# Low part of the feed-forward weights: an accumulating DMA instead of a VectorE subtraction

## The chip, the cores and the metric

The kernel runs on one core of a Trainium2 chip. The metric is device time of one launch in microseconds (us). The engines that matter are TensorE (PE in the rows: matmuls; PEld: its weight loads), VectorE (DVE), ScalarE (ACT), GpSimd (POOL) and SyncE (SP, which only issues DMAs). Each engine works through its own list of instructions in order and meets the others at semaphores.

## What is computed

Two layers of a diffusion transformer on 640 tokens (512 latent, 128 context) of width 1024, in float32: layer 0 mixes tokens with an mLSTM and a Hyena convolution, layer 1 with attention. After each mixer stands a feed-forward block, and that is where the change lies:

```python
def conv_ffn(h, w_up, w_conv, w_down):
    a, g = jnp.split(h @ w_up, 2, axis=-1)
    return (jax.nn.gelu(dwconv3(a, w_conv)) * g) @ w_down
```

Here `w_up` is 1024 x 5632 and `w_down` 2816 x 1024. The input of the block is an RMS norm with conditioning; its output, gated, is added to the residual stream `x`.

## The kernel before

**Exact products.** TensorE multiplies in a reduced format (fp32r). Each float32 operand is therefore split in two such parts, W = Wh + Wl, and a product takes three matmuls: Wh·Xh, Wh·Xl and Wl·Xh. For weights, `split_w` (lines 94 to 99) does this: ScalarE rounds the raw block to Wh (line 97), VectorE subtracts it from the raw block to give Wl (line 98).

**Tiles.** A weight tile is 128 partitions x 1024 float32 (512 KB; 896 columns in the second and third group of `w_down`): eight k-blocks of 128 x 128 for 128 output features. The three stages of a tile are `raw` (four buffers, loaded by SP, line 103), `wh` and `wl` (three buffers each). A tile's buffers come free with its last matmul, so the split of tile i + 3 can start when tile i ends, and is needed two tiles later.

**The block's loops.** `ffn` takes the 22 blocks of 128 inner features in three groups. For each, `up` runs `linear` over the tiles of `w_up` (a and g in turn), then `linear` runs over eight tiles of `w_down`, whose products are added to `x`. Ordinary tiles run one by one through `mm_k` (for each k the three matmuls on both halves of the tokens, the Wl matmul last; lines 118 to 123). Two places differ:

- The head: the first three tiles of `w_up` (`u_0` to `u_2`; a tile u is named by the place of its group's first tile and its own number in it) run together, by halves of the tokens, because the norm before them delivers its result bit by bit. GpSimd makes their low parts. They hold all three `wh` and `wl` buffers until they end, nearly together, so `u_3` can be split only then, and is the next tile that TensorE needs.
- The tail: the last three tiles of `w_down` (`d_5` to `d_7` of the third group) run half by half, so each of them stands only half as long before the next.

While layer 0's block runs, VectorE also computes the conditioning of what follows (`ada_dve`, line 247), from 512 KB loads per step.

**Order.** The order on each engine's list is fixed when the program is built: the framework places instructions by their dependences and its own estimates of time. `conv3`, the GELU, its product and the split of that product (`fcb`, `ge`, `pr`, `G` in the rows) share ScalarE and VectorE with the weight splits.

Of the kernel before, what the change touches and what calls it, by code (L numbers as in the profile page):

```python
# [36 lines left out]
def trunk(ctx: ExitStack, tc: tile.TileContext, I, O, dbg=None, stop=None):  # L37
# [7 lines left out]
    def use_psum(pairs, singles):  # L45
        """the 8 banks of PSUM: so many tiles of two banks and of one"""
        if "es" in psum:
            psum["es"].close()
        es = psum["es"] = ExitStack()
        psum["shape"] = pairs, singles  # L50
        n = psum["n"] = psum.get("n", 0) + 1
        kw = dict(space=bass.MemoryType.PSUM, reuse_waits="tile")
        psum["m"] = es.enter_context(tc.tile_pool(name=f"pm{n}", bufs=pairs, **kw))
        psum["s"] = es.enter_context(tc.tile_pool(name=f"ps{n}", bufs=singles, **kw))
# [7 lines left out]
    def bank(pt, a):  # L62
        """half a of a tile of two banks, or of two tiles of one"""
        return pt[a] if isinstance(pt, tuple) else pt[:, a]

    # ---------------------------------------------------------------- constants and persistent data
# [21 lines left out]
    # ---------------------------------------------------------------- weights: load, exact split  # L88
# [11 lines left out]

    def load_w(src, nm, nk=KT, eng=dve):
        raw = wp.tile([P, 1024], F32, tag="raw", name=nm, bufs=4)
        sp.dma_start(out=raw[:, : nk * P], in_=src)
        wh, wl = split_w(raw, nk * P, nm, eng)
        return wh.rearrange("p (k c) -> p k c", c=P), wl.rearrange("p (k c) -> p k c", c=P)
# [19 lines left out]
    def linear(srcs, done, nm, ks=None, nk=KT, head=2, tail=0, by_half=True, split=SPLIT, filler=None,  # L125
               kcut=None, pre=(), hook=None, spare=False, pooled=(), x_last=False):
        """ks: (k index in the weight tile, xh, xl) in the order of arrival; head: so many first tiles run with
        k outermost; tail: so many last ones finish half by half; spare: the tile after the head in single banks;
        x_last: in the head, the low parts of the tokens come after those of the weights"""
# [4 lines left out]
        while i < n:  # L134
            left = n - i
            g = min(head, left) if i == 0 and head else (tail if tail and left == tail else 1)
            # while a norm holds the vector engine
            eng = pool if i == 0 and head and by_half or i in pooled else dve
# [40 lines left out]
    # tokens on partitions: out[tile] = X[:, tile]^T W, W 512 columns wide  # L179
# [17 lines left out]
    # ---------------------------------------------------------------- adaLN modulation  # L197
# [10 lines left out]
    # on the tensor engine, two blocks (chunk, half of it) of 512 features at once; in four steps  # L208
# [29 lines left out]
    # on the vector engine: rows of W^T times the conditioning vectors; list of steps, one per 128 features  # L238
# [17 lines left out]
    # ---------------------------------------------------------------- RMSNorm (+ adaLN), by halves of the tokens  # L256
    # (start, end, request group) of each half, and overlapping windows of 128 tokens that cover it
# [6 lines left out]
    def rms_steps(nm, a, nrm):  # L264
        """1/rms of the tokens of half a, in every partition of a PSUM tile; in two steps"""
# [18 lines left out]
        # one Newton step of 1/sqrt  # L284
# [26 lines left out]
    def norm_steps(l, which, nrm):  # L311
        """both halves, in seven steps for the end of the product before it"""
# [22 lines left out]

    # ---------------------------------------------------------------- depthwise conv of width 3 along tokens
    # buffers: a column of padding, 512 latent tokens, padding, 128 context tokens, padding
    def halves(pt):
        """both halves of PSUM: the columns that are latent in both, and those latent in the first only"""
        return pt[:, :, 0 : NS - HT], pt[:, :, NS - HT : HT]  # L340

    def conv_parts(buf, d):
        """the same columns of a buffer, moved by d"""
        e = 1 if d > 1 else 0
        return (buf[:, 0 : 2 * HT].rearrange("p (a b) -> p a b", a=2)[:, :, d : d + NS - HT],
                buf[:, e : e + 2 * HT + 2].rearrange("p (a b) -> p a b", a=2)[:, :, NS - HT + d - e : HT + d - e])
# [9 lines left out]
    def tokens(buf):  # L356
        """(slice of the tokens, their columns of a buffer)"""
# [14 lines left out]
    # ---------------------------------------------------------------- ConvFFN  # L372
    def ffn(l, after, hook=None):
        with ExitStack() as es:
# [43 lines left out]
            def up(i0, i1):  # L418
                linear([I["w_up"][l, i // 2, i % 2] for i in range(i0, i1)], lambda i, pt, a: done_up(i0 + i, pt, a),
                       f"u{l}_{i0}_", head=3 if i0 == 0 else 0, filler=filler, spare=i0 == 0)  # L420

            nxt = 0
            for gi, (k0, k1) in enumerate(GROUPS):
                end = 2 * min(k1 + 1, NF)
                if end > nxt:
# [5 lines left out]
                       tail=3 if k1 == NF else 0, hook=hook)  # L431

    # ---------------------------------------------------------------- hyena filters (no data from x)
    def hyena_filters(fl, spectra):
        """in three parts: the loads, the filters, their spectra"""
# [18 lines left out]
        # the decay, where the first of the products with it will be  # L454
# [5 lines left out]
        for j, w in enumerate((w1, w2)):  # L460
# [18 lines left out]
            if j == 0:  # L479
                # sum and difference of the two filters' weights, twice (64 rows each), and their exact split  # L480
# [5 lines left out]
        # high parts of the hidden layer, then low parts  # L486
# [6 lines left out]
        for r in range(5):  # L493
# [8 lines left out]
            if r in (0, 4):  # L502
                # the filter of the future has no tap at 0: half of sum plus difference
# [34 lines left out]
    # ---------------------------------------------------------------- mixers A and B  # L538
    def mixer_ab():
        with ExitStack() as es:  # L540
# [9 lines left out]
            # weight tiles: (v, x1) x 4, x2 x 4, gates, q x 4, k x 4, o x 4  # L550
# [73 lines left out]
            # x holds u, then the convolved u (tiles 0-3), and x2, then y of the hyena (tiles 4-7)  # L624
            def hyena_chunk(j):
# [42 lines left out]
                # context sequence  # L668
# [64 lines left out]
            # running maxima: high parts from rows 0 and 32, low parts 64 rows further; and columns that pick both  # L733
# [7 lines left out]
            def mlstm_gates(pt, rows):  # L741
# [24 lines left out]
                # log_sigmoid(f) = min(f, 0) - log(u) + ((u - 1) - e), u = fl(1 + e)  # L766
# [79 lines left out]
            def head_a(h):  # L846
                q, k = qk[:, h], qk[:, 4 + h]
                # latent sequence
# [33 lines left out]
                # context sequence  # L882
# [19 lines left out]
            def head_b(h):  # L902
# [25 lines left out]
                # norm per head: rstd = exp(-ln(v)/2) and one Newton step  # L928
# [53 lines left out]
    # ---------------------------------------------------------------- mixer C  # L982
    # latent tokens of keys, values and queries go column by column of the grid: token c * 8 + r
    def mixer_c():
        with ExitStack() as es:
# [6 lines left out]
            # context keys of a head, the other head's rows zero  # L992
            kc = [[at.tile([P, P], F32, name=f"kc{b}{e}") for e in range(2)] for b in range(2)]
            # latent keys between 64 columns of padding, the high part twice and the low part once: with the queries
            # as (high, low) they give all products but low times low
            k1 = [[at.tile([P, 640], F32R, name=f"k1{b}{e}") for e in range(2)] for b in range(2)]
            k2 = [[at.tile([P, 640], F32R, name=f"k2{b}{e}") for e in range(2)] for b in range(2)]
            # 64 columns of padding, 512 latent tokens, 64 columns of padding, 128 context tokens
# [13 lines left out]
            # PSUM (rows 0-4 | rows 5-7, context) to column order  # L1012
# [300 lines left out]
def pack(i):  # L1313
# [10 lines left out]
    # (chunk, k pair, half, p, par, 512) and, for the other chunks, transposed (chunk, tile, p, 1024)  # L1324
# [44 lines left out]
    # rpbw[8 b + r, h, 8 a + r2]: bias of query (row r, column c) and key (row r2, column c + a - b - 8)  # L1369
# [45 lines left out]
```

## Time and profile before

| | |
|---|---|
| time, median of 3 runs | 1732.03 us (1731.26 to 1732.91) |
| span of the profiled execution | 1733.2 us |
| TensorE busy | 1676.1 us, 97% |
| VectorE busy | 1052.3 us, 61% |
| ScalarE busy | 672.4 us, 39% |
| GpSimd busy | 142.2 us, 8% |
| DMA moved | 175.62 MB, mean 101 GB/s |

The profiled execution's span lies 1.2 us above the median of the runs. A busy TensorE is not TensorE at its peak, since matmuls overlap: what matters is where its list stands still, and for whom. Idle time of the other engines costs nothing as long as TensorE does not wait for it.

### The profile page before, as it was taken

What the parts mean: (1) busy time and instruction counts of PE and PEld (TensorE: products, weight loads), DVE (VectorE), ACT (ScalarE), POOL (GpSimd) and SP (SyncE); (2) the same over time, 40 slices, a digit from 0 to 9 for tenths busy, and PEclk for the clock granted to TensorE, in tenths of its full rate; (3) what the DMA queues carried; (4) which work ended last, traced back from release to release, by engine and by line L of the source; (5) the groups of instructions that cost most, each with busy time, mean ns of one, the idle gap of its engine ahead of it and who ended that gap; (6) DMA issues with size and microseconds to landing.
All of it is one profiled execution on the core that took longest, in us unless ns stands there. A gap on an engine that the chain in (4) does not pass through costs nothing. (4 is left out here: it accounts for less than half of the span.)

```text
span 1733.2 us, 28191 instructions
## 1 busy us (share of the span) xinstructions
PE 1676.1 (97%) x11434; PEld 1596.5 (92%) x11434; DVE 1052.3 (61%) x2089; ACT 672.4 (39%) x1235; POOL 142.2 (8%) x150
## 2 busy tenths in 40 slices
PE   5999999999999999999997999999999999999997
PEld 2699889899999999999997888998999999999997
DVE  5886656666987677777376555555564433433444
ACT  6323346754432133223245565555343312321332
POOL 3110001101000000000023212120100000000001
PEclk9999999999999999999999999999999999999998
DMA  8334422141454454453213111211222222222211
GB/s 325 117 132 163 160 72 71 48 142 59 140 176 147 146 153 144 154 170 104 79 64 101 60 60 47 65 42 52 74 73 74 73 74 73 71 76 85 69 54 61
DMA packets 57121, 175.62 MB, mean 101 GB/s; under 512 B 7632, under 2 KB 15104, under 8 KB 56736
## 3 DMA queue, kind: packets, MB, share of 16 engines
q1 hardware_dynamic: 56800, 173.66, 31.1%
q8 instruction: 90, 1.47, 0.4%
q14 instruction: 39, 0.32, 0.1%
q0 software_dynamic: 192, 0.17, 0.0%
HBM read 169.61 MB, written 4.20 MB: 100 GB/s over the span
## 5 line engine op out<-in xcount | busy, mean ns | idle before, releaser
L331 DVE SCALAR_TENSOR_TENSOR x<-pd,mod,x 128x320 f32<-128x320 f32 (+2 forms) x144 | 55.1, 434 | 146.7 <-PE pd L122 137.3
L247 DVE CUSTOM_DVE_ANT_0 adj<-adw,cb 128x1024 f32<-128x1024 f32 x112 | 136.7, 1221 | 1.6
L398 DVE TENSOR_TENSOR pr<-pu,ge 128x384 f32<-128x384 f32 x84 | 37.4, 486 | 108.4 <-PE pu L122 107.6
L353 DVE SCALAR_TENSOR_TENSOR fcb<-pu,cwf,fcb 128x384 f32<-128x384 f32 (+1 forms) x176 | 95.8, 549 | 4.1
L388 ACT ACTIVATE ge<-fcb 128x641 f32<-128x641 f32 x44 | 32.6, 742 | 105.4 <-DVE fcb L353 105.4
L306 ACT ACTIVATE XH<-nt,mod 128x192 fp32r<-128x192 f32 (+1 forms) x96 | 39.6, 466 | 44.0 <-DVE nt L302 43.8
L1120 DVE CUSTOM_DVE_ANT_0 s<-pS,bm 128x384 f32<-128x384 f32 x64 | 34.5, 553 | 30.1 <-PE pS L1119 29.0
L307 DVE SCALAR_TENSOR_TENSOR XL<-nt,mod,XH 128x192 fp32r<-128x192 f32 (+1 forms) x96 | 46.4, 521 | 5.0 <-ACT XH L306 4.9
L1021 DVE TENSOR_SCALAR s<-s,nm 128x384 f32<-128x384 f32 (+1 forms) x80 | 46.3, 586 | 1.8
L1019 ACT ACTIVATE s<-s,nm 128x384 f32<-128x384 f32 x64 | 39.2, 612 | 20.3 <-DVE nm L1120 18.3
L350 ACT ACTIVATE fcb<-pu,cwf 128x384 f32<-128x384 f32 x88 | 46.3, 528 | 1.3
L1194 POOL TENSOR_TENSOR fo<-fo,rs 128x320 f32<-128x320 f32 x8 | 6.9, 888 | 469.8 <-ACT rs L1186 469.8
L1134 ACT COPY pTs<-pS 128x384 f32<-128x384 f32 (+1 forms) x80 | 33.7, 434 | 23.4 <-PE pS L1132 22.7
L1132 PE MATMUL pS<-ident,s 128*128 128x128 f32 x208 | 36.3, 281 | 5.8 <-DVE s L1021 5.8
L98 POOL TENSOR_TENSOR qk00l<-qk,qk00h 128x1024 fp32r<-128x1024 f32 x1 | 2.8, 2761 | 461.6 <-DVE rn L288 461.6
L273 ACT ACTIVATE sqn<-x 128x320 f32<-128x320 f32 x56 | 25.3, 466 | 39.4 <-DVE x L331 35.3
L1094 POOL TENSOR_TENSOR bm<-amask,wr 128x768 f32<-128x768 f32 x16 | 30.7, 1918 | 112.6 <-issue 83.9
L302 DVE SCALAR_TENSOR_TENSOR nt<-x,coefA,rbn 128x192 f32<-128x192 f32 (+1 forms) x96 | 36.7, 430 | 3.6 <-PE rbn L294 3.5
L1112 PE MATMUL pS<-k,q 128*128 128x256 f32 x128 | 31.0, 328 | 7.6 <-DVE k L1047 7.1
L400 ACT CAST G<-pr 128x640 fp32r<-128x640 f32 x44 | 31.8, 728 | 13.4 <-DVE pr L398 13.4
L331 DVE SCALAR_TENSOR_TENSOR x<-pop,mod,x 128x320 f32<-128x320 f32 (+2 forms) x36 | 14.4, 433 | 36.7 <-PE pop L122 26.0
L401 DVE TENSOR_TENSOR G<-pr,G 128x640 fp32r<-128x640 f32 x44 | 36.0, 819 | 0.0
(1110 smaller groups left out, 5507.4 us busy)
## 6 DMA issues: line engine op xcount, KB each, us to landing
u<-in_w_up SPq DMA_DIRECT2D x88, 512.0 KB, 3.5
adw<-in_w_adaT SPq DMA_DIRECT2D x56, 512.0 KB, 4.1
wa<-in_w_ada SPq DMA_DIRECT2D x40, 512.0 KB, 5.0
d<-in_w_down SPq DMA_DIRECT2D x32, 448.0 KB, 3.3
qk<-in_w_qkv SPq DMA_DIRECT2D x24, 512.0 KB, 3.5
d<-in_w_down SPq DMA_DIRECT2D x16, 512.0 KB, 3.5
qk<-in_w_ab SPq DMA_DIRECT2D x8, 512.0 KB, 3.5
op<-in_w_oab SPq DMA_DIRECT2D x6, 512.0 KB, 3.4
```

Source lines behind the costliest of these rows:

```text
L247: dve.tensor_tensor_reduce(out=jk, in0=w, in1=cb[:, s], op0=ALU.mult, op1=ALU.add, scale=1.0, scalar=0.0, accum_out=acc[:, k, s : s + 1])
L302: dve.scalar_tensor_tensor(out=t, in0=x[:, k, c0:c1], scalar=coefA[:, n, k, s : s + 1], in1=rb[:, c0 - a * HT : c1 - a * HT], op0=ALU.mult ...
L306: act.activation(out=oh, in_=t, func=AF.Identity, bias=b)
L307: last = dve.scalar_tensor_tensor(out=ol, in0=t, scalar=b, in1=oh.bitcast(F32), op0=ALU.add, op1=ALU.subtract)
L331: r = dve.scalar_tensor_tensor(out=x[:, k, c0:c1], in0=pt[:, h, c0 - h * HT : c1 - h * HT], scalar=mod[:, l, ch, k, s : s + 1], in1=x[:, k ...
L350: act.activation(out=o, in_=i, func=AF.Copy, scale=w[1])
L353: dve.scalar_tensor_tensor(out=o, in0=i, scalar=w[j], in1=o, op0=ALU.mult, op1=ALU.add)
L398: dve.tensor_tensor(out=o, in0=i_, in1=c, op=ALU.mult)
L401: here[0] = dve.tensor_tensor(out=g[:, 1], in0=pr, in1=g[:, 0].bitcast(F32), op=ALU.subtract).ins
L1019: act.activation(out=s, in_=src, func=AF.Exp, scale=-1.0, bias=nm, accum_out=sm)
L1021: dve.tensor_scalar(out=s, in0=s, scalar1=sm, scalar2=None, op0=ALU.mult)
L1132: pe.transpose(pS[:, j * P : (j + 1) * P], s[:, j * P : (j + 1) * P], ident)
```

## The change

A second form of the split, `split_dma`, is used for all tiles of the feed-forward block but the three of the head (82 tiles of `w_up` and 48 of `w_down` in the two layers, 130 in all). ScalarE rounds the raw block to Wh as before, then writes -Wh into `wl`, and a DMA issued by GpSimd adds the raw block in SBUF onto it, in place. VectorE has no part in it any more.

```diff
+    def split_dma(raw, n, nm):
+
+        wh = wp.tile([P, 1024], F32R, tag="wh", name=f"{nm}h")
+        wl = wp.tile([P, 1024], F32R, tag="wl", name=f"{nm}l")
+        act.copy(out=wh[:, :n], in_=raw[:, :n])
+        act.activation(out=wl[:, :n], in_=wh[:, :n].bitcast(F32), func=AF.Copy, scale=-1.0)
+        pool.dma_start(out=wl[:, :n], in_=raw[:, :n], accum_op=ALU.add)
+        return wh, wl
...
-        wh, wl = split_w(raw, nk * P, nm, eng)
+        wh, wl = split_w(raw, nk * P, nm, eng) if eng is not None else split_dma(raw, nk * P, nm)
...
-            eng = pool if i == 0 and head and by_half or i in pooled else dve
+            eng = pool if i == 0 and head and by_half or i in pooled else (None if by_dma else dve)
...
-                       f"u{l}_{i0}_", head=3 if i0 == 0 else 0, filler=filler, spare=i0 == 0)
+                       f"u{l}_{i0}_", head=3 if i0 == 0 else 0, filler=filler, spare=i0 == 0, by_dma=True)
...
-                       tail=3 if k1 == NF else 0, hook=hook)
+                       tail=3 if k1 == NF else 0, hook=hook, by_dma=True)
```

The lists of instructions change with it; lines from 100 on have other numbers afterwards (line 97 becomes 105 here, 122 becomes 131, 350 becomes 359, 273 becomes 282). ScalarE at the end of the head in layer 0, before: `u_0_3h` is Wh of tile `u_3`, `fcb` the convolution's buffer, `pu` a tile's result.

```order
L97 CAST u_0_3h<-u_0_3_4314 128x1024
L350 ACTIVATE fcb_4094<-pu_0_0_4127,cwf_4092 128x2x192
L97 CAST u_0_4h<-u_0_4_4383 128x1024
L350 ACTIVATE fcb_4094<-pu_0_0_4127,cwf_4092 128x2x128
L350 ACTIVATE fcb_4095<-pu_0_2_4129,cwf_4092 128x2x192
L97 CAST u_0_5h<-u_0_5_4452 128x1024
```

The same place now.

```order
L105 CAST u_0_3h<-u_0_3_4314 128x1024
L359 ACTIVATE fcb_4094<-pu_0_0_4127,cwf_4092 128x2x192
L106 ACTIVATE u_0_3l<-u_0_3h 128x1024
L359 ACTIVATE fcb_4094<-pu_0_0_4127,cwf_4092 128x2x128
L359 ACTIVATE fcb_4095<-pu_0_2_4129,cwf_4092 128x2x192
L105 CAST u_0_4h<-u_0_4_4384 128x1024
L359 ACTIVATE fcb_4095<-pu_0_2_4129,cwf_4092 128x2x128
L106 ACTIVATE u_0_4l<-u_0_4h 128x1024
```

Each rounding has a negation (line 106) behind it, one instruction of the convolution between them; the DMA of `u_3` can be issued after the third row. TensorE's list at the first matmuls of `u_3` in layer 0, before; a bracket names the semaphores that a row waits for.

```order
L122 MATMUL pu_0_3_0_4320<-XH,u_0_3h 128x320 [waits Activation_49]
L122 MATMUL pu_0_3_1_4321<-XH,u_0_3h 128x320 [waits PE_49]
L122 MATMUL pu_0_3_0_4320<-XL,u_0_3h 128x320
L122 MATMUL pu_0_3_1_4321<-XL,u_0_3h 128x320
L122 MATMUL pu_0_3_0_4320<-XH,u_0_3l 128x320 [waits DVE_49]
L122 MATMUL pu_0_3_1_4321<-XH,u_0_3l 128x320
```

The same place now.

```order
L131 MATMUL pu_0_3_0_4321<-XH,u_0_3h 128x320 [waits Activation_49]
L131 MATMUL pu_0_3_1_4322<-XH,u_0_3h 128x320 [waits PE_49]
L131 MATMUL pu_0_3_0_4321<-XL,u_0_3h 128x320
L131 MATMUL pu_0_3_1_4322<-XL,u_0_3h 128x320
L131 MATMUL pu_0_4_4391<-XH,u_0_4h 128x320 [waits DVE_49,PE_49,Activation_49]
L131 MATMUL pu_0_4_4391<-XH,u_0_4h 128x320
L131 MATMUL pu_0_3_0_4321<-XH,u_0_3l 128x320 [waits DMASW6_49]
L131 MATMUL pu_0_3_1_4322<-XH,u_0_3l 128x320
```

The first Wl matmul waits for a DMA of GpSimd's queue (DMASW) in place of VectorE, and two matmuls of `u_4` have moved ahead of it. The other matmuls keep their order. ScalarE in the tail of layer 1, before, where `sqfin` are squares for the last norm.

```order
L97 CAST d_2_6h<-d_2_6_16318 128x896
L273 ACTIVATE sqfin_16430<-x 128x320
L97 CAST d_2_7h<-d_2_7_16324 128x896
L273 ACTIVATE sqfin_16433<-x 128x320
L273 ACTIVATE sqfin_16436<-x 128x320
```

The same place now.

```order
L105 CAST d_2_6h<-d_2_6_16446 128x896
L282 ACTIVATE sqfin_16560<-x 128x320
L106 ACTIVATE d_2_6l<-d_2_6h 128x896
L105 CAST d_2_7h<-d_2_7_16453 128x896
L282 ACTIVATE sqfin_16563<-x 128x320
L106 ACTIVATE d_2_7l<-d_2_7h 128x896
L282 ACTIVATE sqfin_16566<-x 128x320
```

The negation of `d_7` stands behind a square. GpSimd's list holds, after the subtractions of the head's three tiles, nothing but the accumulating DMAs of that layer.

## Rows read from the trace of the kernel before

**Rows 1.** The page: busy time of each engine.
```profile
PE 1676.1 (97%) x11434; PEld 1596.5 (92%) x11434; DVE 1052.3 (61%) x2089; ACT 672.4 (39%) x1235; POOL 142.2 (8%) x150
```

**Rows 2.** Stretches (start:end, length, busy PE, PEld, DVE, ACT, POOL, clock, DMA share, GB/s).
```profile
442.00:887.00 445.00, 445.00 (x3035) 444.41 (x3033) 323.34 (x545) 129.61 (x174) 4.88 (x2) 1.00 0.45 139
1274.00:1718.00 444.00, 444.00 (x3032) 444.00 (x3031) 188.21 (x310) 126.44 (x169) 0.00 (x0) 1.00 0.23 71
```

**Rows 3.** Timeline, ordinary tile, layer 1 (start, duration, engine, line, [idle before <- releaser]).
```profile
1399.94 1.05 ACT L97 CAST d_5h<-d 128x1024 fp32r<-128x1024 f32 x1 [5.99 <-PE pd L122]
1401.28 1.22 DVE L98 TENSOR_TENSOR d_5l<-d,d_5h 128x1024 fp32r<-128x1024 f32 x1
...
1413.97 0.63 PEld L122 LDWEIGHTS pd<-G,d_5h 128*128 128x128 f32 x4
```

**Rows 4.** Timeline, end of the head in layer 0.
```profile
439.39 1.05 ACT L97 CAST u_3h<-u 128x1024 fp32r<-128x1024 f32 x1 [1.19 <-PE pu L116]
440.35 0.58 ACT L350 ACTIVATE fcb<-pu,cwf 128x384 f32<-128x384 f32 x1
440.48 1.23 DVE L98 TENSOR_TENSOR u_3l<-u,u_3h 128x1024 fp32r<-128x1024 f32 x1 [1.89 <-ACT u_3h L97]
...
441.94 0.46 PE L122 MATMUL pu<-XH,u_3l 128*128 128x320 f32 x2
442.23 0.46 PE L122 MATMUL pu<-XH,u_3h 128*128 128x320 f32 x2
```

**Rows 5.** Timeline, end of the head in layer 1.
```profile
1271.35 1.05 ACT L97 CAST u_3h<-u 128x1024 fp32r<-128x1024 f32 x1 [1.25 <-PE pu L116]
...
1273.90 0.46 PE L122 MATMUL pu<-XH,u_3l 128*128 128x320 f32 x2
```

**Rows 6.** Timeline, tails of layer 0 and of layer 1.
```profile
866.29 0.94 ACT L97 CAST d_7h<-d 128x896 fp32r<-128x896 f32 x1 [4.75 <-PE pd L122]
...
867.23 0.47 ACT L273 ACTIVATE sqn<-x 128x320 f32<-128x320 f32 x1
867.64 1.08 DVE L98 TENSOR_TENSOR d_7l<-d,d_7h 128x896 fp32r<-128x896 f32 x1
...
872.84 0.31 PE L116 MATMUL pd<-G,d_7l 128*128 128x320 f32 x1
...
1698.25 0.94 ACT L97 CAST d_7h<-d 128x896 fp32r<-128x896 f32 x1 [4.75 <-PE pd L122]
...
1704.80 0.31 PE L116 MATMUL pd<-G,d_7l 128*128 128x320 f32 x1
```

**Rows 7.** DMA issues (queue, count, KB each, median us from issue to landing).
```profile
u<-in_w_up SPq DMA_DIRECT2D x88, 512.0 KB, 3.5
adw<-in_w_adaT SPq DMA_DIRECT2D x56, 512.0 KB, 4.1
...
kctx<-in_k_ctx SPq DMA_DIRECT2D x1, 1024.0 KB, 4.9
...
out_ck<-kc SPq DMA_DIRECT2D x16, 32.0 KB, 1.8
...
selc<-in_k_selc POOLq DMA_DIRECT2D x1, 2.0 KB, 3.1
...
cwq<-in_w_conv_qk POOLq DMA_DIRECT2D x1, 12.0 KB, 5.1
```

**Rows 8.** TensorE around its longest wait, by microseconds (length, busy PE, clock, DMA).
```profile
923.00:924.00 1.00, 0.00 (x0) 0.65 1.23 333
...
925.00:926.00 1.00, 0.54 (x2) 0.50 0.41 164
...
930.00:931.00 1.00, 1.00 (x9) 0.94 0.00 0
```

**Rows 9.** Timeline: the wait that rows 8 show.
```profile
925.46 0.77 PE L1112 MATMUL pS<-k,q 128*128 128x256 f32 x2 [7.11 <-DVE k L1047]
```

**Rows 10.** Timeline: VectorE behind the head of layer 0.
```profile
444.81 3.36 DVE L353 SCALAR_TENSOR_TENSOR fcb<-pu,cwf,fcb 128x256 f32<-128x256 f32 x7
```

More of the change, by code (lines that the diff above doesn't have):

```diff
@@ L125, in linear @@
     def linear(srcs, done, nm, ks=None, nk=KT, head=2, tail=0, by_half=True, split=SPLIT, filler=None,
-               kcut=None, pre=(), hook=None, spare=False, pooled=(), x_last=False):
+               kcut=None, pre=(), hook=None, spare=False, pooled=(), x_last=False, by_dma=False):
         n = len(srcs)
```

## The prediction

> **What bounds the kernel now.** I read the page's busy times first: TensorE 1676.1 of 1733.2 us, VectorE 61%, ScalarE 39%, GpSimd 8% [rows 1]. Then the two stretches that the change touches, from the first tile after each head to the end of the tail: TensorE is busy for 445.00 of 445.00 us in layer 0 and 444.00 of 444.00 in layer 1, at a granted clock of 1.00 [rows 2]. So in the whole feed-forward block TensorE's list is the time, and nothing that VectorE does there is waited for, though it is busy for 323.34 us of layer 0's stretch [rows 2]. Taking work off VectorE can gain nothing in these 889 us. What is left to ask is only whether the new way of making Wl is ever late.
>
> The timeline of an ordinary tile shows how much time there is: d_5 is rounded from 1399.94, VectorE has its low part at 1401.28 + 1.22 = 1402.50, and TensorE's first weight load of it is at 1413.97 [rows 3]. That is 14.03 us (two tiles) after the start of the split, and the first Wl matmul comes another 0.6 us later. At the end of the heads it is otherwise: u_3 is rounded from 439.39, its low part is ready at 440.48 + 1.23 = 441.71, and the first matmul that reads it starts at 441.94 [rows 4]: 0.23 us to spare. In layer 1 the same pair is 1271.35 and 1273.90, again 2.55 us apart [rows 4, 5]. In the tails d_7 is rounded from 866.29 and read at 872.84, and from 1698.25 and 1704.80: 6.55 us apart both times [rows 6].
>
> **Removed: 130 subtractions on VectorE**, 1.22 us each [rows 3], some 150 us in all. Nothing on TensorE's path ended on them in the two stretches, so this is worth 0. In the heads the subtraction of u_3 was on time by 0.23 us; what takes its place is next.
>
> **Added on ScalarE: 130 negations.** They read and write as many elements as the rounding, so I take its 1.05 us (0.94 for 896 columns) [rows 3, 6]; on ScalarE, busy for 129.61 of 445 us [rows 2], they are hidden in ordinary tiles. If they came late they would hold up the rounding of the tile after, which has 14 us. Cost 0, but for the two places where they stand ahead of a late DMA.
>
> **Added on GpSimd: 130 accumulating DMAs.** The trace has no such DMA. Call L the time from its issue to its landing, bounded by the nearest rows. GpSimd's own DMAs, all small, land in 3.1 us (2 KB) to 5.1 us (12 KB, in the crowded start) against 1.8 us for 32 KB on SP's queue [rows 7]. Another 512 KB adds 1.4 us (4.9 for 1024 KB against 3.5 for 512 KB) [rows 7]. An accumulation has to read two blocks and write one. Low end: 3.1 + 1.4 = 4.5 us, as if the second read were free. High end: 5.1 + 3 x 1.4 = 9.3 us, every pass in series on the slowest start. I take the small DMA's 3.1 and two passes: L = 3.1 + 2.8 = 5.9 us, because the reads are what an accumulation doubles, and GpSimd's queue will be as empty as for the 2 KB row. For 896 columns it is 3.1 + 2 x 1.2 = 5.5 us.
>
> [...]
>
> **Ordinary tiles.** Rounding, up to one convolution instruction, negation: the DMA goes out at most 1.05 + 0.58 + 1.05 = 2.7 us after the start of the split and lands at 2.7 + 5.9 = 8.6 us, of 14.6 that there are. Hidden up to L = 11.9 us. The raw buffer is held 6 us longer, so SP's next loads go out later, and the loads of the conditioning queue behind them; raw has four buffers, four tiles or 28 us, so this costs 0 too.
>
> **Heads.** ScalarE does u_3's rounding, the convolution until 440.93, then the negation until 441.98 [rows 4]. The DMA lands at 441.98 + 5.9 = 447.9. TensorE wants it at 441.94 [rows 4]; two matmuls of u_4, which the new list puts ahead, fill 0.3 us. Idle: 447.9 − 441.94 − 0.3 = 5.6 us, or L less 0.3. Behind it everything is shifted, u_4 included: its own DMA goes out two convolution instructions, a rounding and a negation later, about 3.3 us, and a tile takes 7. To this comes the clock. In the longest wait of TensorE, 7.11 us until 925.46 [rows 9], the granted clock fell at about 923.3 (a mean of 0.65 is 0.3 us at 1.00 and 0.7 at 0.50), 5.0 us after the last work, and came back at about 930.1, 4.7 us after work began again [rows 8]. [...] A wait of 5.6 us is just past those 5.0, so I count it: 7.9 us for each head, 15.8 for both. Without the fall it is 11.2.
>
> **Tails.** d_7's rounding ends at 867.23, the square at 867.70, the negation at 868.64; the DMA lands at 868.64 + 5.5 = 874.14 where TensorE wants it at 872.84 [rows 6]: 1.3 us, twice, 2.6 us. For d_6 and d_5 there are 3 and 6 us more, so nothing. The end of the kernel hangs on the last tile's result and moves with it.
>
> **The sum.** 15.8 + 2.6 = 18.4 us onto a span of 1733.2, 1751.6; the profiled span lies 1.2 us above the median of the runs, so 1750.4 us. With the bounds of L: at 4.5 us the heads wait 4.2 us each, without a fall of the clock, and the tails nothing, 8.4 us in all: 1740.4. At 9.3 us the heads cost 9.0 + 2.3 each and the tails (8.8 us for 896 columns) 4.6 each, 31.8 in all: 1763.8.
>
> **Rivals.**
> 1. The DMA engines fill up in layer 0. They are busy for 0.45 there [rows 2], 3.2 us of each 7.04 us tile, since the conditioning is loaded beside the weights (56 loads of 512 KB in all [rows 7]); 3.8 us are free. If an accumulation occupies them for three passes of 1.4 us, 4.2 us, each tile with such a load takes 0.4 us longer: 56 x 0.4 = 22 us, and 1772 us together with the forecast's waits. At four passes, 5.6 us, it is 100 us and more. It decides from 2.7 passes on. For it: nothing in the trace says how fast a DMA adds. Against: layer 1 has 0.23 [rows 2], and two passes fit in both layers.
> 2. [...] Behind the head VectorE runs 3.36 us of convolutions without a gap [rows 10]; if a DMA could not be issued meanwhile, L would grow by as much at the heads: 2 x 3.4 = 6.8 us, 1757 us. For it: both engines would be busy at that moment. Against it: u_3's DMA goes out at 441.98, and that run begins at 444.81, though it moves forward once the subtractions are gone. [...]
> 3. Not slower. A DMA within the chip's SRAM lands as fast as SP's 32 KB, 1.8 us [rows 7]: then each head waits 1.5 us, the tails nothing, and the time is 1732.0 + 3.0 = 1735.0. It decides from L below 2.0 us. Against it: every GpSimd DMA in the trace, with nothing to move, takes 3.1 or more.
>
> **How the numbers follow.** Forecast 73%, 1750.4 us, between 1740.4 and 1763.8 by L. Rival 1 13%, 1772 and up. Rival 2 8%, 1757. Rival 3 6%, 1735. The range leaves out most of rival 3 and the worse half of rival 1: 1738 to 1776. A measurement of this kernel can tell about 0.2% (3.5 us) from no change. Rival 3 gives "same" 5%, and 1% for what I cannot see as a gain; all else is slower: 94%.
>
> **What would show it.** In the changed kernel's trace: TensorE's waits name two long ones at the first u_3 Wl matmul, on the accumulating DMA, of 5 to 6 us, and two of about 1 us at d_7, and no others between 442 and 887 or in layer 1's block; the clock falls to 0.50 behind the heads for 4 to 5 us. VectorE's busy time falls by some 150 us and ScalarE's grows by 130 without any effect. The list of DMA issues gives L itself. Wrong would be: waits at many tiles (L above 12 us, or full DMA engines, a DMA share near 1 in layer 0), waits of VectorE on the conditioning's loads that reach TensorE, or no wait at u_3.

## The result

The changed kernel takes 1747.13 us (median of 4 runs, 1743.91 to 1748.32) against 1732.47 us before on the same chip: a ratio of 1.0079, 95% interval 1.0066 to 1.0093. The forecast was 1750.4 us in a range of 1738 to 1776. The profiled execution has a span of 1746.5 us.

The page of the changed kernel, its busy times and the packets of GpSimd's queue (share of 16 engines' span last), against [rows 1]:

```profile
PE 1680.1 (96%) x11434; PEld 1598.7 (92%) x11434; DVE 913.0 (52%) x1959; ACT 790.6 (45%) x1365; POOL 255.5 (15%) x280
...
q0 software_dynamic: 18912, 66.24, 19.9%
```

VectorE is busy 139 us less, ScalarE 118 us more, and neither shows in the time. The stretches from head to tail, against [rows 2]:

```profile
442.00:893.00 451.00, 446.39 (x3021) 444.93 (x3020) 255.29 (x479) 187.51 (x237) 58.23 (x66) 0.99 0.82 210
1280.00:1731.00 451.00, 446.78 (x3036) 446.08 (x3035) 120.31 (x246) 186.25 (x235) 55.92 (x65) 1.00 0.61 143
```

TensorE now stands still for 4.6 and 4.2 us in these stretches, and the DMA share has gone from 0.45 to 0.82 and from 0.23 to 0.61, that is 0.37 and 0.38 for one accumulation per tile. The end of the head in layer 0, against [rows 4]:

```profile
441.25 1.05 ACT L106 ACTIVATE u_3l<-u_3h 128x1024 fp32r<-128x1024 f32 x1
442.07 0.46 PE L131 MATMUL pu<-XL,u_3h 128*128 128x320 f32 x2
442.88 0.92 POOL L107 DMA_DIRECT2D u_3l<-u  x1 [21.93 <-ACT fcb L359]
445.69 0.87 PE L131 MATMUL pu<-XH,u_4h 128*128 128x320 f32 x2 [3.16 <-DVE fcb L362]
447.41 0.90 PE L131 MATMUL pu<-XH,u_3l 128*128 128x320 f32 x2 [0.85 <-DMA u_3l<-u]
...
456.25 0.46 PE L131 MATMUL pu<-XL,u_4h 128*128 128x320 f32 x2
```

The negation ends at 442.30, GpSimd begins its DMA at 442.88, and the first Wl matmul starts at 447.41, 5.47 us later than the same matmul before [rows 4]. Of that, 0.43 us was there ahead of the head, so the head costs 5.04 us up to here. The two matmuls of u_4 that had moved ahead wait 3.16 us for VectorE, whose line 362 reads TensorE's results (`pu`) out of PSUM; the DMA comes 0.85 us after them. In the kernel before, the XL pair of u_4 stood here:

```profile
448.69 0.46 PE L122 MATMUL pu<-XL,u_4h 128*128 128x320 f32 x2
```

It started at 448.69 there, at 456.25 here: 7.56 us later, so another 2.1 us went in between. That is the clock, here by microseconds (clock third from the end):

```profile
444.00:445.00 1.00, 0.00 (x0) 0.00 (x0) 1.00 (x2) 1.00 (x3) 0.00 (x0) 1.00 0.68 135
445.00:446.00 1.00, 0.31 (x1) 0.34 (x2) 0.96 (x4) 1.00 (x2) 0.06 (x1) 0.84 1.17 233
446.00:447.00 1.00, 0.56 (x2) 0.16 (x1) 0.96 (x2) 0.98 (x2) 0.83 (x1) 0.50 0.80 156
...
451.00:452.00 1.00, 1.00 (x5) 1.00 (x5) 1.00 (x2) 0.00 (x0) 0.33 (x1) 0.50 1.04 369
452.00:453.00 1.00, 1.00 (x7) 1.00 (x6) 0.56 (x2) 0.00 (x0) 0.00 (x0) 0.74 0.92 156
```

It falls from 1.00 to 0.50 at 445.7, 3.2 us after the last work before the wait (until 442.53), and is back at 1.00 from 452.5 on. In between, one pair of matmuls starts 0.53 us after the other (448.11 and 448.64), where it is 0.29 at a clock of 1.00 (441.94 and 442.23 in [rows 4]). The head in layer 1, against [rows 5], where the Wl matmul started at 1273.90:

```profile
1280.93 0.86 POOL L107 DMA_DIRECT2D u_3l<-u  x1 [21.89 <-ACT fcb L359]
1283.79 0.53 PE L131 MATMUL pu<-XH,u_4h 128*128 128x320 f32 x2 [3.16 <-DVE fcb L362]
1285.38 0.90 PE L131 MATMUL pu<-XH,u_3l 128*128 128x320 f32 x2 [1.06 <-DMA u_3l<-u]
```

The tails of both layers, against [rows 6]:

```profile
877.09 0.86 POOL L107 DMA_DIRECT2D d_7l<-d  x1 [5.30 <-ACT d_7l L106]
881.41 0.42 PE L125 MATMUL pd<-G,d_7l 128*128 128x320 f32 x1
...
1713.55 0.86 POOL L107 DMA_DIRECT2D d_7l<-d  x1 [5.30 <-ACT d_7l L106]
1717.72 0.42 PE L125 MATMUL pd<-G,d_7l 128*128 128x320 f32 x1
```

Only 0.2 to 0.4 us are lost there, by the ledger below. One more loss stands in layer 0, four tiles behind the head, at a place that the prediction had counted as 0; the timeline of VectorE and TensorE:

```profile
474.30 1.23 DVE L256 CUSTOM_DVE_ANT_0 adj<-adw,cb 128x1024 f32<-128x1024 f32 x1 [4.08 <-DMA adw<-in_w_adaT]
475.45 0.62 DVE L362 SCALAR_TENSOR_TENSOR fcb<-pu,cwf,fcb 128x384 f32<-128x384 f32 x1
...
477.75 0.53 PE L131 MATMUL pu<-XH,u_7h 128*128 128x320 f32 x2 [0.51 <-DVE fcb L362]
```

VectorE waits 4.08 us for a load of conditioning weights, its convolution comes late, and TensorE waits for that at u_7. SP's waits in the layer's stretch (442 to 890; total us, count, longest) show the load's side of it, first in the kernel before, then in the changed one:

```profile
SPq L244 <- DVE mod L247: 98.4, 49, 3.4
SPq L103 <- DVE u_3l L98: 23.9, 3, 20.8
```

```profile
SPq L112 <- DMA u_3l<-u: 41.9, 3, 26.1
SPq L253 <- DVE mod L256: 34.9, 22, 4.1
```

Before, SP stood ready with a conditioning load 49 times and waited for VectorE to free the buffer (line 244). Now it does so 22 times (line 253). At weight loads it stood before as well, until VectorE's subtraction had read the raw buffer (line 103); now an accumulating DMA reads it (line 112), and all these waits together are 369 us in place of 310. VectorE, which never waited for these loads before, now does:

```profile
DVE adj L256 <- DMA adw<-in_w_adaT: 12.2, 7, 4.1
```

The DMA issues (count, KB, median us from issue to landing), against [rows 7]:

```profile
adw<-in_w_adaT SPq DMA_DIRECT2D x56, 512.0 KB, 6.0
...
u_3l<-u POOLq DMA_DIRECT2D x6, 512.0 KB, 4.7
...
d_7l<-d POOLq DMA_DIRECT2D x4, 448.0 KB, 5.4
```

The accumulations of layer 0 are the slower ones: over its 65, from GpSimd's start to the landing, the median is 6.0 us, over those of layer 1 it is 4.4. The ledger is worked out as the start of the same matmul in the changed kernel less its start in the kernel before, and how that grows at each place (us; head 0 is the head of layer 0, and so on):

```
                         head 0   u_4..u_8   tail 0   head 1   tail 1    sum
changed kernel             7.13       0.74     0.37     6.25     0.22   14.7
```

In all other tiles of the two blocks the difference does not move by 0.1 us. Ahead of the first block it is 0.4 us, and between the blocks it falls by 2.1 us; part of that is the clock, which was 0.57 from 892 to 896 us in the kernel before and stayed at 1.00 behind this tail. The spans of the two profiled executions therefore differ by 13.3 us. That the difference of the medians is 14.7 us, as the ledger, is in part chance: the interval of the ratio leaves 11 to 16 us.

### The profile page after: what moved, and what is told of

Read it like the earlier page. It is cut to its first block, busy times and chain, and to the rows that moved or that the text cites. A ratio compares the mean times of both kernels' runs of the same rounds, so it can differ in the third digit from the quotient of the medians.

```text
span 1746.5 us, 28555 instructions
## 1 busy us (share of the span) xinstructions
PE 1680.1 (96%) x11434; PEld 1598.7 (92%) x11434; DVE 913.0 (52%) x1959; ACT 790.6 (45%) x1365; POOL 255.5 (15%) x280
## 3 DMA queue, kind: packets, MB, share of 16 engines
q0 software_dynamic: 18912, 66.24, 19.9%
## 5 line engine op out<-in xcount | busy, mean ns | idle before, releaser
L256 DVE CUSTOM_DVE_ANT_0 adj<-adw,cb 128x1024 f32<-128x1024 f32 x112 | 136.9, 1223 | 14.4 <-DMA adw<-in_w_adaT 12.2
L1141 PEld LDWEIGHTS pS<-ident,s 128*128 128x128 f32 x208 | 23.6, 141 | 10.6 <-DVE s L1030 8.8
L131 PE MATMUL pd<-G,d_0h 128*128 128x320 f32 x176 | 33.0, 309 | 0.0
L131 PE MATMUL pd<-G,d_2h 128*128 128x320 f32 x176 | 33.0, 309 | 0.0
```

What stands on the lines that cost most here:

```text
L131: pe.matmul(bank(pt, a)[:, : sp_[a][1] - sp_[a][0]], ww[:, kt], xx[:, slice(*sp_[a])], start=(first and n == 0), stop=(last and n == 2))
L256: dve.tensor_tensor_reduce(out=jk, in0=w, in1=cb[:, s], op0=ALU.mult, op1=ALU.add, scale=1.0, scalar=0.0, accum_out=acc[:, k, s : s + 1])
L1141: pe.transpose(pS[:, j * P : (j + 1) * P], s[:, j * P : (j + 1) * P], ident)
```

## The experiments

The theory: the loss is the latency of one DMA at the two heads, between the release of a buffer and its need, with the clock that falls behind it. The rivals: A, the DMA engines are so busy that all tiles pay; B, the work taken off VectorE brings something; C, not the DMA but VectorE's read-out for the pair of u_4 is waited for.

**e_head_dve: u_3 alone by VectorE again.**

```diff
-(None if by_dma else dve)
+(None if by_dma and not (head and i == head) else dve)
```

> u_3 of each layer, the first tile behind the head, gets its low part from VectorE again; the other 128 tiles keep the accumulating DMA. Theory (the whole loss is the DMA's latency at the two heads, 7.1 and 6.3 us of shift in the trace, with 0.3 to 0.4 us at each tail and nothing in ordinary tiles): 1732.5 + 2 x 0.35 = 1733.2 us, between 1731 and 1735, and no idle stretch over 1 us at the first matmuls of u_3. Rival A (the loss is spread over all the tiles, by DMA engines that are 0.82 busy in layer 0's stretch): still 1744 to 1747. Rival B (the 139 us taken off VectorE give something back that the heads hid): below 1730.

Measured: 1734.44 us against 1733.14, ratio 1.0003 (0.9995 to 1.0012). The head's loss is gone with 2 of the 130 DMAs, while the DMA share stays at 0.82 in layer 0's stretch, so A falls for the size of this change. The small ones remain: 0.52 us at u_7, 0.46 and 0.22 us in the tails. Of B nothing is seen.

**e_only_u3: the other way round.**

```diff
-(None if by_dma else dve)
+(None if by_dma and head and i == head else dve)
```

> The other way round: only u_3 of each layer uses the accumulating DMA, the other 128 tiles are subtracted by VectorE as before. Theory (heads alone): 1747.1 - 0.7 for the two tails = 1746.4 us, between 1743 and 1748, with the DMA share of the two stretches back at 0.45 and 0.23. Rival A (spread over all tiles): below 1736. If L depends on how busy the DMA engines are, u_3's DMA lands sooner than the 4.5 us from GpSimd's start that it took with all tiles, and the time is lower by twice that difference; theory: 4.5 us again.

Measured: 1748.57 us, ratio 1.0088 (1.0073 to 1.0102). That is 0.6 us above the expected range, and the interval overlaps that of the changed kernel. Two DMAs bring the whole loss. The stretch in layer 0, and the DMA's landing:

```profile
442.00:893.00 451.00, 446.66 (x3028) 445.82 (x3027) 322.17 (x545) 130.26 (x174) 3.94 (x3) 0.99 0.45 138
```

```profile
u_3l<-u POOLq DMA_DIRECT2D x2, 512.0 KB, 4.5
```

With a share of 0.45 in the stretch the DMA of u_3 takes as long as with 0.82, 4.5 us: the latency at the heads doesn't come from crowding. The losses at u_7 and in the tails are 0.00 and 0.01 us here, so those do belong to the other 128.

**e_fill: TensorE kept at work through the wait.** In `mm_k`, for u_3's first block, behind the Wh·Xl pair:

```diff
+            for q in range(fill if n == 1 else 0):
+                pe.matmul(bank(pt, q % 2)[:, HT:512], wh[:, kt], xh[:, 0 : 512 - HT], start=False, stop=False)
```

> All tiles by DMA as in the changed kernel; behind the Wh.Xl pair of u_3's first block, TensorE gets 44 matmuls of 192 columns more whose results nobody reads (320 columns take 0.147 us in a row, so some 3.9 us), in the time in which it would stand still for u_3's DMA. They also keep the pair of u_4 from moving ahead of u_3's first Wl matmul. Theory (of the heads' shift of 7.1 and 6.3 us 4.9 each are idle time and the rest, 2.2 and 1.4, the granted clock that falls behind it): the clock stays at 1.00, the first Wl matmul still starts 4.9 us late and waits for the DMA, and the time is 1747.1 - 3.6 = 1743.5 us, between 1741 and 1745. Rival C (what is waited for is not the DMA but VectorE's read-out of PSUM for the u_4 pair that had moved ahead, 3.16 us in the trace): the Wl matmul starts as soon as the 44 are done, without a wait for the DMA, and the time is 1741 or less. If the clock is not what costs the rest: 1747 again.

Measured: 1746.58 us, ratio 1.0078 (1.0065 to 1.0091), which can't be told from the changed kernel and lies outside the expected 1741 to 1745. By the time alone the clock would be worth nothing; the trace says where the gain went. The timeline of its head in layer 0 and of u_7, and one microsecond behind the head:

```profile
442.23 5.03 PEld L134 LDWEIGHTS pu<-XH,u_3h 128*128 128x128 f32 x44
442.37 5.06 PE L134 MATMUL pu<-XH,u_3h 128*128 128x192 f32 x44
...
447.41 0.30 PEld L131 LDWEIGHTS pu<-XH,u_3l 128*128 128x128 f32 x2 [0.16 <-DMA u_3l<-u]
...
464.48 1.23 DVE L258 CUSTOM_DVE_ANT_0 adj<-adw,cb 128x1024 f32<-128x1024 f32 x1 [8.11 <-DMA adw<-in_w_adaT]
...
476.86 0.54 PE L131 MATMUL pu<-XH,u_7h 128*128 128x320 f32 x2 [1.61 <-DVE fcb L364]
```

```profile
449.00:450.00 1.00, 1.00 (x8) 1.00 (x8) 0.30 (x1) 1.00 (x3) 0.00 (x0) 1.00 1.16 143
```

The pair of u_4 no longer stands ahead, and the Wl matmul starts at 447.41 as in the changed kernel, on the DMA. So the DMA alone is late enough for the whole wait, and C does not explain the changed kernel. The test of C is close in layer 0: the 44 matmuls took 5.06 us where 3.9 had been worked out, and the last of their weight loads ended only 0.16 us ahead of the next one, which waited for the DMA. In layer 1 the Wl matmul waits 0.56 us for the DMA behind them. The clock stays at 1.00, and head 0 costs 5.13 us in place of 7.13: the clock is worth 2.0 us there, near the 2.2 expected. In head 1 it is only 0.53 us, since the DMA took 0.7 us longer (5.16 us from GpSimd's start in place of 4.45). But u_7 now costs 1.99 us in place of 0.74 and the tail of layer 0 0.83 in place of 0.37. Of the 2.0 us that the clock gave in layer 0, these two took 1.7 back, behind VectorE's wait for its loads, 8.11 us this time, and a later DMA in the tail.

**e_wl4: the split of u_3 begun during the head.** Four `wl` buffers, three `raw`, and the negation made from the raw block, ahead of the rounding:

```diff
-        act.copy(out=wh[:, :n], in_=raw[:, :n])
-        act.activation(out=wl[:, :n], in_=wh[:, :n].bitcast(F32), func=AF.Copy, scale=-1.0)
+        act.activation(out=wl[:, :n], in_=raw[:, :n], func=AF.Copy, scale=-1.0)
         pool.dma_start(out=wl[:, :n], in_=raw[:, :n], accum_op=ALU.add)
+        act.copy(out=wh[:, :n], in_=raw[:, :n])
```

> All 130 tiles by DMA, but the DMA no longer waits for the head's buffers: wl has four buffers (raw three instead of four, for the space), and ScalarE makes the negated high part from the raw block directly, ahead of the rounding. So u_3's low part can be made some 18 us earlier, while the head runs. Theory (the loss is latency between the release of a buffer and its need, not work): the waits at the heads go, those at the tails too, 1732.5 us, between 1731 and 1735, at the same DMA shares of about 0.8 and 0.6. Rival A (occupied DMA engines): still 1744 or more. Rival D (one raw buffer fewer, or a negation within the norm on ScalarE's list, costs as much as is won): 1736 to 1745.

Measured: 1735.64 us against 1733.14, ratio 1.0013 (1.0004 to 1.0022). All 130 DMAs are there, the shares are 0.81 and 0.61, and the heads and tails cost nothing (0.01 us at most). The timeline of u_3's split in layer 0, and of u_7:

```profile
417.40 1.04 ACT L105 ACTIVATE u_3l<-u 128x1024 fp32r<-128x1024 f32 x1
418.75 0.92 POOL L106 DMA_DIRECT2D u_3l<-u  x1 [0.16 <-issue]
...
468.64 0.53 PE L131 MATMUL pu<-XH,u_7h 128*128 128x320 f32 x2 [0.90 <-DVE fcb L362]
```

The DMA goes out at 418.75 in place of 442.88, and nobody waits for it: for the heads and tails the theory holds. The time lies between its range (to 1735) and rival D's (from 1736), and the interval puts it 0.7 to 3.8 us above the kernel before. In the profile 1.13 us of that stand in the block, at u_7.

**e_copy: the same DMAs, copying.**

```diff
-        pool.dma_start(out=wl[:, :n], in_=raw[:, :n], accum_op=ALU.add)
+        pool.dma_start(out=wl[:, :n], in_=raw[:, :n].bitcast(F32R))
```

> The same DMAs as in the changed kernel, but they copy the raw block over the negated high part and don't add (Wl becomes W, so the products are left wrong). Theory of the prediction's term (an accumulation is one pass more than a copy, 1.4 us for 512 KB): the DMA lands 1.4 us sooner at the heads, some 3.1 us from GpSimd's start instead of 4.5; the DMA shares of the two stretches fall from 0.82 and 0.61 to about 0.64 and 0.42; and the time is 1747.1 - 2 x 1.4 - about 1 of clock = 1743 us. Rival (adding costs a DMA nothing that a copy does not): the same landing, shares and time, 1747.

Measured: 1740.88 us against 1731.38, ratio 1.0050 (1.0034 to 1.0067). From its page, the queue and the issues:

```profile
q0 software_dynamic: 18912, 66.24, 10.5%
...
u_3l<-u POOLq DMA_DIRECT2D x6, 512.0 KB, 2.8
```

Per DMA the queue is occupied for 10.5% of 1737.6 us over 130, 1.40 us; accumulating it is 19.9% of 1746.5 over 130, 2.67 us: 1.9 times as long. The shares of the two stretches are 0.65 and 0.43, where 0.64 and 0.42 had been expected. The landing at the heads is 1.5 us sooner (2.9 us from GpSimd's start against 4.5 and 4.4), near the 1.4 us expected for the pass that an accumulation has more; over all six it is 1.9 us. Yet head 0 still costs 3.40 us, and head 1 4.93 with the clock. Its timeline in layer 1, and one microsecond behind it:

```profile
1273.47 0.56 POOL L107 DMA_DIRECT2D u_3l<-u  x1 [21.89 <-ACT fcb L359]
1276.33 0.53 PE L131 MATMUL pu<-XH,u_4h 128*128 128x320 f32 x2 [3.16 <-DVE fcb L362]
1276.70 0.46 PE L131 MATMUL pu<-XH,u_3l 128*128 128x320 f32 x2
```

```profile
1279.00:1280.00 1.00, 1.00 (x5) 0.50 0.73 287
```

The Wl matmul has no wait of its own any more: the pair of u_4 ahead of it waits 3.16 us for VectorE, and that ends last. So C lies right under the theory: in the changed kernel the DMA is last, but by 0.85 and 1.06 us only, and with this order of the matmuls a DMA faster by more than that would gain nothing further on the wait. The same wait of 3.16 us stands at head 0; there the clock stays at 1.00, behind head 1 it is 0.50 from 1278 to 1281.

**e_twice and e_half_more: the load on the DMA engines.** Both add behind the DMA:

```diff
+        pool.dma_start(out=wl[:, :n], in_=raw[:, :n], accum_op=ALU.add)      (e_twice)
+        pool.dma_start(out=wl[:, :512], in_=raw[:, :512], accum_op=ALU.add)  (e_half_more)
```

> Every low part gets the raw block added twice, by two DMAs one behind the other (the products are left wrong): the latency and the load on the DMA engines of 130 tiles doubled. Latency alone (ordinary tiles hide up to 11.9 us; two DMAs land some 9 to 10 us after the negation): the two heads and tails wait about 4.5 us more each, 1747.1 + 4 x 4.5 = 1765 us, and nothing else waits. If the busy share is what the DMA engines can give (0.37 for one accumulation per tile in layer 0, so 0.82 + 0.37 = 1.19 there, 0.61 + 0.38 = 0.99 in layer 1): layer 0's stretch of 451 us becomes 1.19 times as long, 86 us more, about 1850 us in all, with waits at ordinary tiles of layer 0 and almost none in layer 1.

> As the run before, but the second DMA adds only half of the block (512 of 1024 columns; the products are left wrong). Latency alone: the heads and tails wait some 3 us more each, 1759 us. With the shares as the limit: 0.82 + 0.19 = 1.01 in layer 0, just full, 0.80 in layer 1: some 10 to 20 us more than that, waits at ordinary tiles in layer 0 only. So this run and the one before say how far the changed kernel is from the end of what the DMA engines can do.

Measured: e_twice 1920.38 us, ratio 1.1097 (1.1071 to 1.1124); e_half_more 1785.66 us, ratio 1.0316 (1.0297 to 1.0335). The stretches of layer 0 and 1 of e_twice, then of e_half_more:

```profile
440.00:990.00 550.00, 472.72 (x2957) 460.00 (x2957) 249.52 (x459) 180.55 (x224) 113.78 (x130) 0.94 0.95 232
1393.00:1888.00 495.00, 454.62 (x2957) 441.71 (x2956) 113.75 (x226) 181.39 (x226) 113.71 (x130) 0.98 0.89 197
```

```profile
440.00:914.00 474.00, 445.81 (x2950) 439.34 (x2951) 249.70 (x459) 180.15 (x224) 113.47 (x130) 0.98 0.94 235
1316.00:1761.00 445.00, 436.83 (x2955) 435.39 (x2953) 113.77 (x226) 181.66 (x226) 112.34 (x130) 0.99 0.83 183
```

By the ledger, ordinary tiles of layer 0 lose 98 us in e_twice and 29.5 in e_half_more. Ordinary tiles of layer 1 lose 45 us in e_twice and 0.0 in e_half_more. Both times are above what was expected, 1850 us and some 1770 to 1780. The 45 us in layer 1, at a share of 0.89, were not expected at all. GpSimd's timeline there shows their cause:

```profile
1506.31 0.91 POOL L107 DMA_DIRECT2D d_0l<-d  x1
1513.01 0.86 POOL L108 DMA_DIRECT2D d_0l<-d  x1 [5.79 <-DMA d_0l<-d]
1513.68 1.08 POOL L107 DMA_DIRECT2D d_1l<-d  x1
1521.49 0.86 POOL L108 DMA_DIRECT2D d_1l<-d  x1 [6.73 <-DMA d_1l<-d]
```

The second DMA of a tile (line 108) waits until the first (line 107) has landed, and GpSimd's list, which is in order, stands there; the next tile's first DMA goes out right behind it. From the first such DMA of this block at 1393.77 to the last at 1877.50 that is 7.56 us for each of 64 tiles, and 59 of the 65 tiles' first DMAs find GpSimd without a pause before them. TensorE's 444 us [rows 2] are 6.83 us for each of 65 tiles. The difference over 64 tiles, 47 us, is about the loss; at a share of 0.89 the DMA engines were not full. In e_half_more only 9 of the 65 first DMAs of layer 1 find GpSimd so, and nothing is lost.

In layer 0 the two causes stand together. In e_twice the DMA engines are busy for 0.95 x 550 = 522 us there, which would not fit into the changed kernel's 451 us on any list: rival A is real at two accumulations per tile. In e_half_more they are busy for 0.94 x 474 = 446 us, which just would, and 50 of the 65 first DMAs go out without a pause on GpSimd; which of the two costs the 29.5 us is not shown. So for one DMA per tile no run tells where above 0.82 the DMA engines begin to cost TensorE time.

**e_adw_pool: the conditioning's loads on another queue.** In e_wl4, `sp.dma_start(out=w, in_=I["w_adaT"]...)` becomes `pool.dma_start`.

> The variant with four wl buffers (no wait at the heads), but the 56 loads of the conditioning weights go out on GpSimd's queue, not on SP's, where they stand behind loads of weights that wait for a raw buffer. In that variant TensorE still lost 1.13 us at u_7 of layer 0, behind VectorE, which had waited 8.7 us in all for these loads. Theory (the loads go out late, because the accumulating DMA holds the raw buffer and SP's list is worked off in order): that 1.13 us goes, VectorE's waits for these loads fall well below 8.7 us, and the time is some 1734.5 us. Rival (the loads themselves land late, 5.7 to 6.0 us instead of 4.1, because the DMA engines are 0.81 busy): the waits stay or grow.

Measured: 1737.76 us against 1731.38, ratio 1.0029 (1.0019 to 1.0039). In its profile TensorE loses nothing in either block, u_7 included. But VectorE waits no less for the loads, 9.8 us in all, so the expectation is met by half. This kernel and that of e_wl4 ran once more with a profile:

> The kernel of e_adw_pool once more, for another profile: eight of its nine runs had a mean granted clock of 0.991 or 0.992 and took 1736.2 to 1738.5 us, while the profiled one had 0.994 and took 1733.4, less than the lower clock explains by nothing that its trace shows. If this profile has the lower clock: the stretches at 0.50 lie outside the feed-forward blocks, at the start or behind the 7.1 us wait in layer 1's attention, and the block's TensorE is as in the first profile, without a wait at the heads, at u_7 or in the tails. If a wait in the block differs from run to run, it shows at u_7 of layer 0. Expected: 1736 to 1738 us with one stretch more at 0.50 outside the blocks.

> The kernel of e_wl4 once more, for another profile: its profiled run took 1732.9 us at 0.994, the median of its eleven runs is 1735.6. Expected: 1734 to 1737 us, no wait at the heads and in the tails again, some 1 us at u_7 of layer 0, and any difference to the first profile in stretches at 0.50 outside the feed-forward blocks. If the 1.13 us at u_7 grows to 2 us or more here, VectorE's wait for the conditioning's loads varies from run to run.

Measured: 1736.7 and 1734.0 us. In e_wl4 the loss at u_7 is 1.14 us again and all else 0. In e_adw_pool a wait of the same kind has come back two tiles later, with 1.27 us in the ledger:

```profile
484.00 0.53 PE L131 MATMUL pu<-XH,u_9h 128*128 128x320 f32 x2 [1.04 <-DVE fcb L362]
```

So the place of the loads decides where VectorE waits, but not that it does: they land in 5.7 to 6.0 us in place of 4.1 on either queue. On GpSimd's list, too, they stand in order, behind accumulating DMAs. How much of the loss is late issue and how much late landing is not settled. The other 1.9 of the 3.3 us between e_adw_pool's two profiles came ahead of the blocks, where the clock was 0.81 and 0.63 from 36 to 42 us in the second and 1.00 in the first (mean over the whole execution 0.993 and 0.994); that part was as expected.

That most runs of e_adw_pool lie 5 to 7 us above the median of the kernel before is explained in part. TensorE lost 0 and 1.27 us in its two profiles. Behind the last work on the output, GpSimd's (until 1729.19 and 1724.95 us), the kernel before (span 1733.2) ends after 4.0 us, e_adw_pool (span 1731.6) after 6.65, in both of its profiles; e_wl4, which differs from it in that queue alone, ends after 4.4. That is 2.6 us, with up to 1.3 in layer 0. What that end consists of stays open.

Where each kernel lost, from the ledger (us, worked out as above):

```
                         head 0   u_4..u_8   tail 0   head 1   tail 1
changed kernel             7.13       0.74     0.37     6.25     0.22
e_only_u3                  7.33       0.00     0.01     6.12     0.00
e_fill                     5.13       1.99     0.83     5.72     0.23
e_copy                     3.40       0.00     0.00     4.93     0.00
e_head_dve                 0.00       0.52     0.46     0.00     0.22
e_wl4                      0.00       1.13     0.01     0.00     0.00
e_adw_pool                 0.00       0.00     0.00     0.00     0.00
```

No version beats the kernel before. TensorE was busy for every one of its 889 us in the two stretches [rows 2], so the best that another way of making Wl can do there is to cost nothing.

## Why the prediction was right

**That VectorE's relief is worth 0: right.** 139 us less work on it (some 150 foretold), and in the blocks TensorE gained nothing by it (e_head_dve, e_wl4).

**That ordinary tiles hide the DMA: right for TensorE's own wait**, in all 120 or so tiles away from heads and tails. In layer 1 even one and a half accumulations per tile are hidden (0.0 us lost in e_half_more).

**The heads: right in place, the DMA's terms somewhat high.** From the end of the negation to the landing 5.9 us were foretold. It was 447.41 - 442.30 = 5.1 us. The two passes, 2.8 us, were 2.67 (the queue's share in the changed kernel; a copy's one pass is 1.40). What was too high is the start, taken from the 2 KB row with 3.1 us [rows 7]: from GpSimd's own start at 442.88 the whole took 4.5 us, so some 1.9 are left for all that isn't the passes, and 0.58 between the negation and GpSimd. The copy, at 2.8 us with a pass of 1.40, leaves 1.4. That an accumulation occupies the DMA engines 1.9 times as long as a copy fits the prediction's two passes. But both queues count the same 18912 packets and 66.24 MB, and whether the 1.27 us more are the second read, as it argued, is not shown.

**What the wait at the heads is: wrong in part.** The prediction let the two matmuls of u_4 fill 0.3 us and named one wait of 5 to 6 us, on the DMA, as its sign. The trace has two: 3.16 us at the pair of u_4, for VectorE's read-out of PSUM, and only then 0.85 and 1.06 us for the DMA. The prediction did not ask what the pair waits for. Its price was right all the same because the DMA comes last; with a copy it is the pair, and the 3.16 us stay (e_copy).

**The clock: the right size, for a reason that does not hold.** The 2.3 us foretold for each head were the author's estimate, about half of the 4.7 us at 0.50 of [rows 8], and no run shows them: 2.0 were measured by e_fill in layer 0, and in layer 1 1.3 us lie between the Wl matmul and the XL pair of u_4, where the clock was 0.50 from 1285.4 to 1288.8. The prediction counted the fall because a wait of 5.6 us is longer than the 5.0 of [rows 8]. But the clock of the changed kernel fell 3.2 us after the last work in layer 0 and 4.7 us after it in layer 1 (at 1285.4, last work until 1280.63), and in e_copy the same wait of 3.16 us had a fall behind it at one head and none at the other. That it came at both heads here was in part luck.

**The tails: the right place, the wrong size.** 1.3 us each were foretold, 0.37 and 0.22 measured. The term that was too large is L for 896 columns, 5.5 us: from GpSimd's start at 877.09 to the matmul at 881.41 it is 4.3 us, and some 0.3 us lie between the negation and that start. The wait of 1.3 was a small difference of large terms, and the 3.1 us start was in it.

**What the prediction set to 0 and was not: the raw buffer, and with it SP's list.** It said that raw is held 6 us longer and that four buffers, 28 us, cover that. In layer 0 SP stands longer at weight loads for it (369 us in place of 310), the conditioning loads behind them go out with less lead (22 of them wait for their buffer in place of 49), they also land in 6.0 us in place of 4.1, and VectorE, whose list is in order, stands at its products with them (12.2 us in all). Which of the two, the later issue or the longer landing, costs more is not shown. TensorE got 0.74 us of it, up to 2.0 in e_fill. The prediction had named this wait as a sign of being wrong; it is there, and small.

The sum of 18.4 us was thus 14.7: 15.8 for the heads became 13.4, 2.6 for the tails 0.6, and 0.7 were counted as 0.

**The rivals.** Rival 1 (full DMA engines) does not decide here: one accumulation occupies 2.67 us, 1.9 passes of 1.4, where the prediction had it decide from 2.7 passes. At one and a half times that, 2.9 passes, layer 0's ordinary tiles lose 29.5 us; at 3.8 passes 98 us. The prediction had 22 us at three passes and over 100 at four, but that these are close confirms little, since GpSimd's list was full as well in those two runs. Rival 2 (a DMA of GpSimd can't be issued while VectorE works): the issue took 0.92 us at 442.88, with VectorE at work from 442.75 to 447.11, and 0.86 us in the tail at 877.09, with VectorE idle. No wait of 3 us is there. Rival 3 falls: the DMA takes 4.5 us, and a copy still 2.8.

## What to carry to other kernels

An engine that nobody waits for can be relieved of 139 us for nothing: look first at who waits, then ask only whether the new way is ever late, and that is at the places where a buffer is released just before its content is needed. A DMA in the place of an engine's instruction needs its latency, 4.5 us at the heads here, hidden by an earlier release (one buffer more, and the input of the step taken from where it is ready first, as in e_wl4), or that one tile left to the engine (e_head_dve). Price it twice, by its latency at such places and by its occupation against the free share of the DMA engines (0.82 was harmless for TensorE but for 0.7 us; at two accumulations per tile the work of layer 0 no longer fits), and look at everything that stands behind it on an in-order list: the loads behind a longer-held buffer (VectorE waited 12.2 us for them), and the issuing engine itself where one DMA waits for another (45 us in layer 1 of e_twice).

## What was not expected of the hardware

- Adding in a DMA from SBUF to SBUF occupies the 16 DMA engines for 2.67 us, a copy for 1.40 us, as the mean of 130 DMAs of 448 and 512 KB (changed kernel, e_copy). At the head of layer 0 GpSimd's issue takes 0.92 us for the accumulation and 0.61 for the copy.
- 44 matmuls of 192 columns took 5.06 us, 0.115 each, where 0.088 had been worked out from 320 columns in 0.147; the row of their weight loads has 5.03 us for the 44, as long as the matmuls themselves (e_fill).
- Two dependent DMAs per tile filled GpSimd's list before they filled the DMA engines: 7.56 us per tile and 45 us lost at a DMA share of 0.89 (e_twice, layer 1).
- The same wait of 3.16 us on TensorE had a fall of the granted clock to 0.50 behind it at one head and none at the other (e_copy).
